# Leading groups side by side, gate products in another PSUM tile, gla levels in one call, values two pairs at a time

## The chip, the cores and the metric

The kernel runs on one core of a Trainium2 chip. The time is the device time of one execution in microseconds; a run's number is the median of its rounds. The chip's engines appear under these names: TensorE (PE, its weight loads PEld), VectorE (DVE), ScalarE (ACT), GpSimd (POOL) and SyncE (SP, which here only issues transfers).

## What is computed

Two transformer blocks in fp32 over 256 tokens of width 2048. In short form:

```python
# block 1
q_a, k_a, v_a, q_b, k_b, v_b, f_b = split(rmsnorm(x) @ w_in)
o_a = sliding window attention with sinks (16 heads of 64, 2 kv heads, window 128)
c   = cumsum(log_sigmoid(f_b + b_forget))               # the forget gates, 16 heads
o_b = softmax(q_b k_b^T / 8 + c[t] - c[s], causal) v_b  # forgetting attention, 16 heads
x   = x + rmsnorm(concat(rmsnorm(o_a), rmsnorm(o_b)) @ w_out)
x   = x + rmsnorm((gelu(gate) * val) @ w_down),  gate, val = causal_dwconv(rmsnorm(x) @ w_up)
# block 2
sb_q, sb_k, sb_v, sb_g, gla_q, gla_k, gla_v, gla_r, gla_g, sgu_u, sgu_v, sgu_g = split(rmsnorm(x) @ w_in_2)
o_sb  = stick-breaking attention          # 8 heads of 128
o_gla = gated linear attention            # 4 heads, keys of 64, decay from gla_r
o_sgu = gelu(u) * (tril(w_s) @ rmsnorm(gelu(v)) + b_s)
x = x + (rmsnorm_per_head(concat(o_sb, o_gla, o_sgu)) * silu(gates)) @ w_out_2
x = x + cross_attention(rmsnorm(x), rmsnorm(mem))
return rmsnorm(x, final_norm)
```

## The kernel before

Activations are kept transposed, with channels on partitions. All weights pass through one stream, `WeightStream`: a sub is a raw tile `wr` of 128 x up to 1024, loaded by SyncE in the order of the list `units` (L559 and on), four raw tiles deep. ScalarE makes the high half `wh` (L110), VectorE the low half `wl` (L117), three subs ahead, and `release` issues the next load once the low half is done. A wide sub carries four k-tiles of a group of 256 output channels; `ws_sub` multiplies them k-tile by k-tile, for each of the two output tiles one product of the low weights (L248, 256 columns: high inputs only) and one of the high weights (L249, 512 columns: high and low inputs). A group's first k-tile uses L245 and L246. `as_chunk` does the narrow groups with L281 to L283. The low halves of the inputs are made by VectorE in L225, and PSUM tiles `P` (two) hold the groups' sums until `join` has read them.

The order is written by hand. Everything beside the stream is a generator: `Kern.step`, called after each k-tile, counts down the generators' waits, and `yield n` means n k-tiles of pause. Within an engine instructions run in the order in which they were written, so an instruction that waits holds up all behind it on its engine.

Block 1: `attn64` makes scores into PSUM tiles `S` (L475), adds the bias on VectorE (L483), takes the exponentials (L416), transposes the weights through the one tile `T` (L434) and copies them out (L437); `values` multiplies them with V for a pair of heads into the one tile `O` (L452, L453), copies that (L455) and squares it (L463) for the group norm (`group_norm_split`, whose sum over partitions is `rms`, L328). GpSimd makes the window bias (`alibi`, L715) and scales the queries and keys (`scaled`, L317). `fox_gates` computes c by a product with a triangle U (L734 to L736), transposes it (L742), sends it to DRAM as `negc` and loads it back on all partitions into B6 and B7 (L750), which `fox_bias` reads later.

Block 2: `block2_mix` begins with two groups, `gq` and `gk` (weights w_gqk, eight subs), while the norm's residual pass still makes the inputs R (L788, L789), their high (L217) and low (L225) halves. `gla` then forms the decayed products level by level (`level`, nine levels): four products (L1124) for each of two diagonal blocks into two S tiles, then a masked copy by VectorE (L1130). The cross attention ends with the output projection; `block2_tail` sums squares by columns (`by_square`, `rms_tok`, `by_row`), multiplies R in eight steps (L1372) and stores it.

Of the kernel before, what the change touches and what calls it, by code (L numbers as in the profile page):

```python
# [16 lines left out]
P = 128  # L17
# [131 lines left out]
class Kern:  # L149
# [151 lines left out]
    def join(self, ps, ntile=2):  # L301
# [3 lines left out]
        e2 = self.t((P, 2, S), "e2")  # L305
# [48 lines left out]

    def by_square(self, sqs):

        ps = self.p("T")
        for half in range(2):
            for i, sq in enumerate(sqs):
                self.nc.tensor.matmul(ps[:, half:half + 1], sq[:, half * P:(half + 1) * P], self.ones[:, 0:1],  # L360
                                      start=i == 0, stop=i == len(sqs) - 1)
        return ps[:, 0:2]
# [39 lines left out]
    def attn64(self, pairs, qf, kf, vf, bias, sink, oraw, acc, pts, n_pts, ready, vready=None):  # L402
# [38 lines left out]
        def values():  # L441

            n = len(pairs)
            order = [2 * (h // 2) for p in pairs for h in p]
            order = sorted(set(order), key=lambda h: max(i for i, p in enumerate(pairs) if h in p or h + 1 in p))
            for i, h0 in enumerate(order):
                while not (h0 in weighted and h0 + 1 in weighted and (vready is None or self.ready[vready])):
                    yield 1
                o = self.p("O")
                for h in (h0, h0 + 1):  # L450
                    r, pt = (h % 2) * 64, weighted.pop(h)
                    nc.tensor.matmul(o[r:r + 64, 0:S], vf(h, 0), pt[:, 0:S], start=True, stop=False)  # L452
                    nc.tensor.matmul(o[r:r + 64, P:S], vf(h, 1), pt[:, S:S + P], start=False, stop=True)  # L453
                n_done[0] += 2
                nc.scalar.activation(oraw()[:, h0 // 2, :], o[:, 0:S], AF.Copy)  # L455
                if i < 2:
                    sq = acc[i]
                elif i < n - 1:
                    sq = self.t((P, S), "tc")
                else:  # L460
                    nc.vector.tensor_tensor(out=acc[0], in0=acc[0], in1=acc[1], op=ALU.add)
                    sq = acc[1]
                nc.scalar.activation(sq, o[:, 0:S], AF.Square)  # L463
                if 2 <= i < n - 1:
                    nc.gpsimd.tensor_tensor(out=acc[i % 2], in0=acc[i % 2], in1=sq, op=ALU.add)
                yield 1
# [32 lines left out]
    def group_norm_split(self, oraw, acc, gi, dst):  # L499
# [3 lines left out]
        rb = self.rms(acc, 1024, "rb")  # L503
# [20 lines left out]
    def setup(self):  # L524
# [37 lines left out]
        wide("w_gqk")  # L562
# [9 lines left out]
        nc.gpsimd.dma_start(self.gain0, a["gain0"])  # L572
        self.exp_tables()

    def block1_mix(self):
# [9 lines left out]
        for kt in range(2):  # L585
            nc.sync.dma_start(R[:, kt, :], a["xT"][:, kt, :])
            self.ws.dma()
# [11 lines left out]
        acca = [V[0][:, o + i * S:o + (i + 1) * S] for i in (1, 2)]  # L599
        accb = [V[1][:, o + P + i * S:o + P + (i + 1) * S] for i in (0, 1)]  # L600
# [72 lines left out]
        def fox():  # L673
# [12 lines left out]
            yield from self.group_norm_split(ob[0], accb, 8, dst)  # L686

        for g in range(4):
            ps = self.ws_group(x) if g else psq
            self.push(self.scaled(ps, qa[:, 2 * g:2 * g + 2, :], rq, "swa", 4))  # L690
            if g == 0:
# [3 lines left out]
                    self.group_norm_split(oa, acca, 0, dst), fox()), 8)  # L695
# [23 lines left out]
    def fox_gates(self, V):  # L719
# [13 lines left out]
        ps = self.p("T")  # L733
# [5 lines left out]
        yield 4  # L739
        ps = self.p("T")  # L740
# [5 lines left out]
        nc.gpsimd.dma_start(dr, ct)  # L746
        self.N = [self.t((P, 8, S), "B6"), self.t((P, 8, S), "B7")]
        for i in range(2):
            src = dr[8 * i:8 * i + 8, :].rearrange("a b -> (a b)").partition_broadcast(P)
            nc.gpsimd.dma_start(self.N[i].rearrange("p a b -> p (a b)"), src)  # L750
# [201 lines left out]
    def scaled_late(self, ps, dst, which):  # L952
        e = self.join(ps)
# [5 lines left out]
    def block2_mix(self):  # L959
# [6 lines left out]
        for dst, w in ((gq, "rq"), (gk, "rb")):  # L966
            ps = self.ws_group(x)
            self.push(self.scaled_late(ps, dst, w))
# [92 lines left out]
    def gla(self, G0, G1, gr, V, tg):  # L1061
# [41 lines left out]
        def level(l):  # L1103
# [17 lines left out]
            for s_, t_, slot in ((0, 0, 0), (1, 1, 2)) if l < 8 else ((0, 1, 1),):  # L1121
# [385 lines left out]
```

## Time and profile before

| | us |
|---|---|
| median of 3 runs (lowest to highest) | 1664.18 (1663.37 to 1664.45) |
| the profiled execution | 1668.66 |
| its span | 1667.0 |
| PE busy | 1638.9 (98%) |
| PEld busy | 1434.2 (86%) |
| DVE busy | 1084.0 (65%) |
| ACT busy | 934.8 (56%) |
| POOL busy | 329.5 (20%) |

The profile is one execution, and its span is what lies between its first and last instruction. A busy share is an average over the span; idle places and the granted clock are read from windows and timelines of their stretch. In a timeline row the bracket tells how long the engine was idle before the instruction and what released it.

### The profile page before, as it was taken

The page shows a single profiled execution, that of the slowest core. Times are in us where ns is not written, and L with a number is a line of the kernel's source. Part 1 is how long each engine was busy: PE and PEld are TensorE (multiplying, and loading weights), DVE is VectorE, ACT ScalarE, POOL GpSimd, SP SyncE. Part 2 cuts the span into 40 slices and gives each one's busy share as a digit, 9 for nine tenths or more (in the row PEclk, how much of TensorE's full clock was granted, in tenths as well). Part 3 has the DMA queues.
Part 4 walks back from the last instruction along what each step waited for, and adds up shares of the span by engine and source line. Part 5 has one row for each costly group of instructions (what it writes and reads, how often), then busy time and mean ns, then how long its engine had stood idle before and what let it go on. Part 6 is the DMA issues. An engine that isn't in the chain of part 4 may idle for free. (4 is left out here: it accounts for less than half of the span.)

```text
span 1667.0 us, 25018 instructions
## 1 busy us (share of the span) xinstructions
PE 1638.9 (98%) x9458; PEld 1434.2 (86%) x9458; DVE 1084.0 (65%) x1578; ACT 934.8 (56%) x1470; POOL 329.5 (20%) x270
## 2 busy tenths in 40 slices
PE   9899999999999999999999999998999999999997
PEld 8688887888888888888888888887989888888896
DVE  5677775568777777777774444448664655666766
ACT  6565565746555555555554444445545666655655
POOL 0344642211122212221220000001110322210112
PEclk9999999999999999999999999999999999999998
DMA  8545443746555555555555555654645544456652
GB/s 305 178 129 173 158 163 130 234 150 210 194 188 193 186 192 189 192 186 194 187 193 190 189 185 190 207 180 159 189 141 177 186 144 158 168 189 207 224 165 106
DMA packets 88393, 303.29 MB, mean 182 GB/s; under 512 B 9888, under 2 KB 10320, under 8 KB 87760
## 3 DMA queue, kind: packets, MB, share of 16 engines
q1 hardware_dynamic: 86976, 296.53, 52.2%
q0 software_dynamic: 1152, 4.76, 0.9%
q8 instruction: 74, 1.21, 0.3%
q14 instruction: 47, 0.39, 0.1%
q10 hardware_dynamic: 144, 0.40, 0.1%
HBM read 298.75 MB, written 2.90 MB: 181 GB/s over the span
## 5 line engine op out<-in xcount | busy, mean ns | idle before, releaser
L117 DVE TENSOR_TENSOR wl<-wr,wh 128x1024 fp32r<-128x1024 f32 (+4 forms) x546 | 687.9, 1262 | 337.3 <-ACT wh L110 336.5
L110 ACT ACTIVATE wh<-wr 128x1024 fp32r<-128x1024 f32 (+4 forms) x546 | 562.0, 1030 | 533.1 <-PE P L249 366.5
L249 PE MATMUL P<-X,wh 128*128 128x512 f32 x1852 | 649.3, 392 | 0.0
L249 PE MATMUL P<-B,wh 128*128 128x512 f32 x1668 | 590.2, 395 | 2.6 <-ACT B L217 1.4
L248 PE MATMUL P<-X,wl 128*128 128x256 f32 x1852 | 522.9, 282 | 1.4 <-ACT wh L110 1.3
L248 PE MATMUL P<-B,wl 128*128 128x256 f32 x1668 | 473.3, 284 | 1.9 <-DVE wl L117 1.9
L249 PEld LDWEIGHTS P<-X,wh 128*128 128x128 f32 x1852 | 348.5, 188 | 73.6
L249 PEld LDWEIGHTS P<-B,wh 128*128 128x128 f32 x1668 | 314.3, 188 | 74.3 <-DVE B L225 1.9
L248 PEld LDWEIGHTS P<-X,wl 128*128 128x128 f32 x1852 | 348.7, 188 | 7.0 <-issue 2.2
L248 PEld LDWEIGHTS P<-B,wl 128*128 128x128 f32 x1668 | 314.7, 189 | 5.8 <-DVE wl L117 1.7
L900 POOL TENSOR_TENSOR e<-e,rb 128x512 f32<-128x512 f32 x44 | 94.6, 2151 | 397.2 <-DVE e L309 382.3
L309 DVE TENSOR_TENSOR e<-P,e 128x512 f32<-128x512 f32 x93 | 64.2, 691 | 154.1 <-ACT e L308 150.0
L399 POOL TENSOR_TENSOR acc<-acc,tc 128x512 f32<-128x512 f32 x18 | 26.7, 1482 | 275.3 <-ACT tc L398 275.3
L281 PE MATMUL P<-wh,B 128*128 128x412 f32 (+2 forms) x192 | 68.7, 358 | 0.0
L905 ACT ACTIVATE tc<-e,cols 128x256 f32<-128x256 f32 x88 | 48.3, 597 | 34.1 <-POOL e L900 34.1
L282 PE MATMUL P<-wl,B 128*128 128x412 f32 (+2 forms) x192 | 65.0, 339 | 0.0
L283 PE MATMUL P<-wh,B 128*128 128x412 f32 (+2 forms) x192 | 65.0, 338 | 0.0
L308 ACT ACTIVATE e<-P 128x512 f32<-128x512 f32 x93 | 54.1, 582 | 9.0 <-PE P L249 6.9
L910 DVE SCALAR_TENSOR_TENSOR tc<-e,cols,tc 128x254 f32<-128x254 f32 x88 | 42.6, 484 | 3.1
L245 PE MATMUL P<-X,wh 128*128 128x512 f32 x116 | 43.5, 398 | 0.0
L908 DVE SCALAR_TENSOR_TENSOR tc<-e,cols,tc 128x255 f32<-128x255 f32 x88 | 41.8, 475 | 1.8 <-ACT tc L905 1.8
L281 PEld LDWEIGHTS P<-wh,B 128*128 128x128 f32 x192 | 36.1, 188 | 2.7 <-issue 0.3
(310 smaller groups left out, 1609.7 us busy)
## 6 DMA issues: line engine op xcount, KB each, us to landing
wr<-w_up SPq DMA_DIRECT2D x176, 512.0 KB, 4.4
wr<-w_down SPq DMA_DIRECT2D x88, 512.0 KB, 4.5
wr<-w_out SPq DMA_DIRECT2D x64, 512.0 KB, 4.5
wr<-w_qkb SPq DMA_DIRECT2D x32, 512.0 KB, 3.7
wr<-w_sb SPq DMA_DIRECT2D x32, 512.0 KB, 3.6
wr<-w_gate SPq DMA_DIRECT2D x32, 512.0 KB, 3.7
wr<-w_v SPq DMA_DIRECT2D x24, 412.0 KB, 3.2
wr<-w_v SPq DMA_DIRECT2D x16, 414.0 KB, 3.6
```

The source lines that it names most:

```text
L110: k.nc.scalar.activation(h[:, :n], src, AF.Copy)
L117: self.k.nc.vector.tensor_tensor(out=l[:, :n], in0=src, in1=h[:, :n].bitcast(F32), op=ALU.subtract)
L245: mm(o, wh, xf, start=True, stop=False)
L248: mm(o[:, 0:S], wl, xk[:, 0, :], start=False, stop=False)
L249: mm(o, wh, xf, start=False, stop=last)
L281: mm(o, xh, hh, start=kt == 0, stop=False)
L282: mm(o, xh, ll, start=False, stop=False)
L283: mm(o, xl, hh, start=False, stop=kt == KT - 1)
L308: nc.scalar.activation(e1[:, t0:t1, :], p[:, 0:t1 - t0, S:2 * S], AF.Copy)
L309: nc.vector.tensor_tensor(out=e2[:, t0:t1, :], in0=p[:, 0:t1 - t0, 0:S], in1=e1[:, t0:t1, :], op=ALU.add)
L900: nc.gpsimd.tensor_tensor(out=e, in0=e, in1=self.rb2(self.r2), op=ALU.mult)
L905: nc.scalar.activation(y[:, t, :], e[:, t, :], AF.Identity, scale=w(t, 2), bias=w(t, 3))
```

## The change

- *Gates.* `fox_gates` uses tile O for both products; the pauses are 12, 8, 4 and 6 k-tiles; its three transfers are issued by SyncE.
- *Values.* `values` takes two pairs of heads at a time in one O tile of 2 x 256, with one copy and one square of 512 columns; the norm then sums three tiles of squares (`sq_att`).
- *Head of block 2.* The eight subs of gq and gk alternate by four k-tiles, both P tiles are held, and the joins write into the destination.
- *Levels.* Both diagonal blocks of a level go into the same two S tiles in one run of eight products, with one masked copy of 512 columns per tile.
- *Tail and start.* The final norm uses `rms` with six tiles of squares instead of column sums; the scaling of the last four tiles of R moves behind it. The first gain is loaded by SyncE after the first input.

```diff
@@ join
-        e2 = self.t((P, 2, S), "e2")
+        e2 = self.t((P, 2, S), "e2") if e2 is None else e2
@@ values
-            for i, h0 in enumerate(order):
...
-                o = self.p("O")
-                for h in (h0, h0 + 1):
...
-                nc.scalar.activation(oraw()[:, h0 // 2, :], o[:, 0:S], AF.Copy)
...
-                nc.scalar.activation(sq, o[:, 0:S], AF.Square)
-                if 2 <= i < n - 1:
-                    nc.gpsimd.tensor_tensor(out=acc[i % 2], in0=acc[i % 2], in1=sq, op=ALU.add)
+            for i in range(0, n, 2):
+                hs = order[i:i + 2]
...
+                o = self.p("O").rearrange("p (a b) -> p a b", a=2)
+                for j, h0 in enumerate(hs):
+                    for h in (h0, h0 + 1):
+                        r, pt = (h % 2) * 64, weighted.pop(h)
+                        nc.tensor.matmul(o[r:r + 64, j, 0:S], vf(h, 0), pt[:, 0:S], start=True, stop=False)
+                        nc.tensor.matmul(o[r:r + 64, j, P:S], vf(h, 1), pt[:, S:S + P], start=False, stop=True)
...
+                nc.scalar.activation(oraw()[:, hs[0] // 2:hs[1] // 2 + 1:d, :], o, AF.Copy)
+                sq = acc if i == 0 else self.t((P, 2, S), "tc")
+                nc.scalar.activation(sq, o, AF.Square)
+                if i == n - 2:
+                    self.fold(acc, nc.vector)
+                    self.sq_att = [acc[:, 0, :], sq[:, 0, :], sq[:, 1, :]]
+                elif i:
+                    nc.gpsimd.tensor_tensor(out=acc, in0=acc, in1=sq, op=ALU.add)
@@ group_norm_split
-        rb = self.rms(acc, 1024, "rb")
+        rb = self.rms(self.sq_att, 1024, "rb")
@@ units
-        wide("w_gqk")
+        for i in range(2):
+            for half in range(2):
+                for g in range(2):
+                    units.append((a["w_gqk"][2 * g + i][:, 1024 * half:1024 * half + 1024], [1024], False))
...
-        nc.gpsimd.dma_start(self.gain0, a["gain0"])
@@ block1_mix
+            if kt == 0:
+                nc.sync.dma_start(self.gain0, a["gain0"])
@@ fox_gates
-        ps = self.p("T")
+        ps = self.p("O")
...
-        yield 4
-        ps = self.p("T")
+        yield 8
+        ps = self.p("O")
...
-        nc.gpsimd.dma_start(dr, ct)
+        yield 4
+        nc.sync.dma_start(dr, ct)
+        yield 6
...
-            nc.gpsimd.dma_start(self.N[i].rearrange("p a b -> p (a b)"), src)
+            nc.sync.dma_start(self.N[i].rearrange("p a b -> p (a b)"), src)
@@ block2_mix
-        for dst, w in ((gq, "rq"), (gk, "rb")):
-            ps = self.ws_group(x)
-            self.push(self.scaled_late(ps, dst, w))
+        pss = [self.big(), self.big()]
+        for i in range(0, KT, 4):
+            for ps, dst, w in ((pss[0], gq, "rq"), (pss[1], gk, "rb")):
+                self.ws_sub(ps, x, list(range(i, i + 4)), (0, KT - 1))
+                if i == KT - 4:
+                    self.push(self.scaled_late(ps, dst, w, dst))
@@ level
-            for s_, t_, slot in ((0, 0, 0), (1, 1, 2)) if l < 8 else ((0, 1, 1),):
...
-                    nc.tensor.matmul(pss[h % 2][:, h // 2 * P:(h // 2 + 1) * P], rows(k_, h)[:, s_ * P:(s_ + 1) * P],
...
-                        nc.vector.copy_predicated(a2, gm[:, l, :].unsqueeze(1).broadcast_to([P, 2, P]), ps3)
+            blocks = ((0, 0), (1, 1)) if l < 8 else ((0, 1),)
...
+                    c = (h // 2 * n + i) * P
+                    nc.tensor.matmul(pss[h % 2][:, c:c + P], rows(k_, h)[:, s_ * P:(s_ + 1) * P],
...
+                    nc.vector.copy_predicated(a2[:, :, 0:3:2, :],
+                                              gm[:, l, :].unsqueeze(1).unsqueeze(1).broadcast_to([P, 2, 2, P]), ps4)
@@ resid_evac
+            if g < 6:
+                self.sq_acc(acc, Rg, g == 0)
+            else:
+                self.sq_last = self.t((P, 2, S), "tc")
+                nc.scalar.activation(self.sq_last, Rg, AF.Square)
+                return
@@ block2_tail
-        rc, dg = self.rms_tok(self.by_square(sqs), D, "rb1c")
-        nc.scalar.activation(Rt, Rt, AF.Copy, scale=self.col("final", 15))
-        rb = self.t((P, S), "rb")
-        nc.vector.tensor_copy(rb, self.by_row(dg))
+        sqs[2:2] = [self.sq_last[:, 0, :], self.sq_last[:, 1, :]]
+        rb = self.rms(sqs, D, "rb")
+        for t in range(12, KT):
+            nc.scalar.activation(self.R[:, t, :], self.R[:, t, :], AF.Copy, scale=self.col("final", t))
```

Three places in the order of the instructions. A row is a line of the kernel, the operation, the tile written and the tiles read, with the number that tells one tile of a name from the next. First GpSimd at the gates; `td` is the window bias, `B_33` the buffer of a group of queries. Before:

```order
L715 TENSOR_SCALAR td_663<-cp_70 128x384
L715 TENSOR_SCALAR td_665<-cp_70 128x384
L746 DMA negc<-acc_691 16x256
L750 DMA B_71_697<-negc 128x2048
L750 DMA B_72_698<-negc 128x2048
L317 TENSOR_TENSOR B_33_490<-e_67_673,rq_479 128x512
L715 TENSOR_SCALAR td_770<-cp_70 128x384
```

After (the bias is L711 now):

```order
L711 TENSOR_SCALAR td_663<-cp_70 128x384
L711 TENSOR_SCALAR td_665<-cp_70 128x384
L317 TENSOR_TENSOR B_33_490<-e_67_673,rq_479 128x512
L711 TENSOR_SCALAR td_765<-cp_70 128x384
L711 TENSOR_SCALAR td_767<-cp_70 128x384
```

The queries' product now stands directly behind the two biases. The three transfers stand on SyncE, among the loads of weights; SyncE after:

```order
L89 DMA wr_716<-w_qa 128x1024
L89 DMA wr_779<-w_v 128x780
L743 DMA negc<-acc_733 16x256
L89 DMA wr_813<-w_v 128x780
L748 DMA B_83_849<-negc 128x2048
L748 DMA B_84_850<-negc 128x2048
L89 DMA wr_888<-w_v 128x780
```

Between the small transfer and the broadcasts stands one load of w_v, and behind the broadcasts the next. On TensorE at the gates, without the weight products and the repeats between; `fz` are the gates, `sm` the softmax weights. Before:

```order
L736 MATMUL T_630<-fz_516,cp_70 128x16
L475 MATMUL S_647<-B_17_95,B_33_490 128x128
L475 MATMUL S_648<-B_17_95,B_33_490 128x256
L434 MATMUL T_667<-ident_65,sm_569 128x128 x3
L742 MATMUL T_688<-ident_65,fc_634 16x128 x2
L434 MATMUL T_701<-ident_65,sm_574 128x128 x3
```

After:

```order
L732 MATMUL O_630<-fz_516,cp_70 128x16
L467 MATMUL S_647<-B_17_95,B_33_490 128x128
L467 MATMUL S_648<-B_17_95,B_33_490 128x256
L425 MATMUL T_667<-ident_65,sm_569 128x128 x3
L425 MATMUL T_688<-ident_65,sm_574 128x128 x3
L738 MATMUL O_730<-ident_65,fc_634 16x128 x2
```

The gates' products write O, and no transpose of `sm` stands behind them on the same tile. Last, TensorE at the head of block 2, the first product of each of the eight subs; the tiles B read are the inputs, four k-tiles in each, and P the sums. Before:

```order
L245 MATMUL P_10677<-B_588_10565,wh_10613 128x512
L248 MATMUL P_10677<-B_589_10566,wl_10638 128x256
L248 MATMUL P_10677<-B_590_10567,wl_10668 128x256
L248 MATMUL P_10677<-B_591_10568,wl_10704 128x256
L245 MATMUL P_10792<-B_588_10565,wh_10731 128x512
L248 MATMUL P_10792<-B_589_10566,wl_10760 128x256
L248 MATMUL P_10792<-B_590_10567,wl_10785 128x256
L248 MATMUL P_10792<-B_591_10568,wl_10819 128x256
```

After:

```order
L245 MATMUL P_10645<-B_576_10533,wh_10581 128x512
L245 MATMUL P_10646<-B_576_10533,wh_10605 128x512
L248 MATMUL P_10645<-B_577_10534,wl_10636 128x256
L248 MATMUL P_10646<-B_577_10534,wl_10673 128x256
L248 MATMUL P_10645<-B_578_10535,wl_10701 128x256
L248 MATMUL P_10646<-B_578_10535,wl_10729 128x256
L248 MATMUL P_10645<-B_579_10536,wl_10754 128x256
L248 MATMUL P_10646<-B_579_10536,wl_10783 128x256
```

Each tile of inputs is now used for both sums before the next one is read.

## Rows read from the trace of the kernel before

**Rows 1.** Windows: stretch, length, then busy PE, PEld, DVE, ACT, POOL, clock, DMA.

```profile
60.00:80.00 20.00, 15.13 (x80) 11.87 (x78) 8.91 (x29) 7.57 (x20) 8.32 (x8) 0.83 0.52 189
...
1140.00:1160.00 20.00, 18.96 (x95) 16.58 (x96) 15.46 (x24) 11.84 (x19) 0.00 (x0) 0.86 0.37 115
```

**Rows 2.** Timeline of POOL, 57 to 72 us: start, duration, instruction, idle before, releaser.

```profile
60.12 2.42 POOL L715 TENSOR_SCALAR td<-cp 128x384 f32<-128x384 f32 x2 [2.92 <-DVE mx L483]
63.59 0.59 POOL L746 DMA_DIRECT2D negc<-acc  x1 [1.04 <-DVE acc L744]
68.73 1.14 POOL L750 DMA_DIRECT2D B<-negc  x2 [4.56 <-ACT mx L419]
69.89 1.27 POOL L317 TENSOR_TENSOR B<-e,rq 128x512 f32<-128x512 f32 x1
```

**Rows 3.** Timeline of PE, 55 to 80 us, the waits and the work behind.

```profile
59.47 0.55 PE L434 MATMUL T<-ident,sm 128*128 128x128 f32 x3 [1.41 <-DVE fc L738]
...
63.34 0.55 PE L434 MATMUL T<-ident,sm 128*128 128x128 f32 x3 [1.71 <-DVE acc L744]
...
71.21 1.65 PE L475 MATMUL S<-B,B 64*128 64x128 f32 x8 [3.16 <-POOL B L317]
```

**Rows 4.** DMA issues: queue, count, KB each, median us to landing.

```profile
B<-negc POOLq DMA_DIRECT2D x2, 1024.0 KB, 8.2
```

**Rows 5.** Timeline of SP, then ACT, 68 to 92 us.

```profile
75.88 14.66 SPq L89 DMA_DIRECT2D wr<-w_v  x4
...
90.95 0.84 ACT L110 ACTIVATE wh<-wr 128x780 fp32r<-128x780 f32 x1
```

**Rows 6.** Timeline of PE: value blocks, norm, end of the group norm, gla block.

```profile
247.26 0.66 PE L452 MATMUL O<-B,B 128*64 128x256 f32 x4
...
248.06 0.39 PE L248 MATMUL P<-B,wl 128*128 128x256 f32 x1
...
249.82 0.66 PE L452 MATMUL O<-B,B 128*64 128x256 f32 x4 [0.80 <-ACT B L463]
...
265.05 1.02 PE L328 MATMUL O<-B,ones 128*128 128x256 f32 x4
...
278.00 0.36 PE L248 MATMUL P<-X,wl 128*128 128x256 f32 x1 [1.26 <-ACT wh L110]
...
1198.27 0.72 PE L1124 MATMUL S<-B 64*128 64x128 f32 x8
...
1198.92 0.45 PE L281 MATMUL P<-wh,B 128*128 128x414 f32 x1
```

**Rows 7.** Groups by shape, 1180 to 1262 us: busy, mean ns.

```profile
L1130 DVE COPY_PREDICATED B<-B,S 128x256 f32<-128x256 uint32 x32 | 12.4, 443 | 0.0
```

**Rows 8.** Timeline of DVE at the head of block 2: low weights.

```profile
1131.14 1.22 DVE L117 TENSOR_TENSOR wl<-wr,wh 128x1024 fp32r<-128x1024 f32 x1
...
1142.09 1.21 DVE L117 TENSOR_TENSOR wl<-wr,wh 128x1024 fp32r<-128x1024 f32 x1
```

**Rows 9.** Timeline of PE at the head of block 2.

```profile
1132.41 0.39 PE L248 MATMUL P<-B,wl 128*128 128x256 f32 x1 [1.40 <-DVE wl L117]
...
1158.41 0.39 PE L249 MATMUL P<-B,wh 128*128 128x512 f32 x1
...
1158.76 0.40 PE L249 MATMUL P<-B,wh 128*128 128x512 f32 x1
...
1158.99 0.35 PE L281 MATMUL P<-wh,B 128*128 128x414 f32 x1
```

**Rows 10.** Timeline: the norm of rms (DVE), then the tail (PE, DVE).

```profile
1119.86 0.42 DVE L337 SCALAR_TENSOR_TENSOR rb<-rb,rb 128x256 f32<-128x256 f32 x1
...
1653.37 0.61 PE L360 MATMUL T<-ones,acc 128*128 128x1 f32 x4 [0.80 <-POOL acc L399]
...
1658.25 4.90 DVE L1372 TENSOR_TENSOR R<-R,rb 128x512 f32<-128x512 f32 x8
```

**Rows 11.** Timeline of ACT at the start.

```profile
6.04 0.51 ACT L217 ACTIVATE X<-R,gain 128x256 fp32r<-128x256 f32 x1 [3.53 <-DMA gain<-gain]
```

## What I predicted

> **What bounds the kernel now.** I read the busy shares first: TensorE is at work in 98% of the span, and no other engine passes 65%. So a change pays only where it shortens an idle place of TensorE, a stretch at half clock, TensorE's own work, or the two ends. The windows come next: the clock falls in two inner places, around 70 us and 1140 us [rows 1]. The reader is to see that both follow idle places of TensorE, and to look in the timeline for who ended each. In the first block the gates' PSUM tile T and then GpSimd hold TensorE up [rows 2, 3]; at the head of block 2 it is VectorE, which makes the low parts of the weights [rows 8, 9].
>
> The sum is made against the profiled execution, 1668.66 us. The median of the three runs, 1664.18, is 4.5 lower; the result is moved by that.
>
> **Gates of the forgetting attention.** Before, TensorE waits 1.41 us at 59.47 and 1.71 us at 63.34, both times because tile T, which the attention's transposes want, still holds the gates' products until VectorE has read them, and 3.16 us at 71.21 for the queries that GpSimd scales in L317 [rows 3]. GpSimd issues the small transfer at 63.59, then stands in its queue until that lands, issues the two broadcasts at 68.73 and comes to L317 only at 69.89 [rows 2]. After these waits the clock is at half: a mean of 0.83 over 20 us is 6.8 us at 1.2 GHz [rows 1], and all but its first half microsecond, 6.3 us, is work of TensorE from 71.21 on [rows 3]: at full speed 3.15.
> After: the gates use O, and the transposes wait only for their own weights. I leave 0.4 us at each of the first two places for those (an estimate: VectorE's scaling of them follows TensorE's arrival closely, and T no longer delays it). On GpSimd L317 stands right behind the products that end at 62.54 [rows 2], so with its 1.27 us the queries are there at 63.8, before TensorE reaches them (about 65). So 1.41 + 1.71 + 3.16 − 0.8 = 5.5 us of waits, and 3.15 of clock: −8.65. The end that costs less is the waits alone, −5; the other is all of it, −9.5.
>
> The three transfers now stand in SyncE's queue among the weight loads. Who waits behind them: the small one waits for nothing new, but the broadcasts wait for its landing, and behind them stands the third load of w_v. SyncE's loads of w_v are issued from 75.88 on, and the first of them is converted by ScalarE at 90.95 [rows 5]; a load lands in 3 to 4 us, so some 12 us are free. The broadcasts take 8.2 us to land [rows 4]. Cover holds: cost 0; if the cover were gone it would be up to 8.2. Their readers come at about 140 us.
> The Trainium skill (DMA: Bandwidth & Descriptors, "Queues, rings and completion order") says that the DMA engines take turns between the rows of different issuers but take one issuer's descriptors in ring order. By it, the 2 MB that used to share the engines with the weights now go ahead of a load: a delay of up to the whole landing, not half of it. By either the sum stays, as the slack is longer; no row here has a transfer of that size ahead of the weights. What it would do if the slack is shorter is rival 5.
>
> **Values two pairs at a time.** A block of four value products takes from 247.26 to 248.06, 0.81 us, and the products on either side stand 0.1 us further apart than usual; the eight records by themselves would need 0.65 [rows 6]. So about 0.25 to 0.35 per block is the switch between kinds of products. Sixteen blocks become eight: −2.0. The three squares that now enter each of the two norms are one matmul more each, 0.43 from the row at 265.05 (four records and the switch, 1.02) : +0.86. In the second attention two waits shrink: 0.80 at 249.82, for the read of O [rows 6], becomes one longer read of 512 columns (ScalarE goes from 0.39 to an estimated 0.6) met half as often, and the 1.26 at 278.00 [rows 6], at the end of the group norm's chain, becomes about 0.7, as the norm starts 2 us earlier. Together −1.2. Sum −2.4; bounds: +0.5 if the longer reads stall TensorE at each of the eight blocks by 0.4, −3.5 if switching is worth 0.35.
>
> **Leading groups of block 2.** A sub (four k-tiles of a group) is eight pairs of products at 0.35 (1158.41 to 1158.76), 2.79 us [rows 9]. VectorE is busy without a break there: it makes the inputs and the low weights of the subs, whose ends are 1132.36, 1136.00, 1139.26 and 1143.30 (first and last of four in rows 8: start plus duration). Before, the q group wants all sixteen k-tiles in 11 us and waits four times, for low weights and for inputs, 4.4 us; and the clock is at half from 1138.9 to 1145.8 [rows 1, 9]. After, q and k use the same four k-tiles in turn, so the next four inputs are wanted every 5.6 us instead of 2.8, and only the low weights are waited for: the second sub starts at 1132.41 as now, the third at 1136.05 (wait 0.85), the fourth at 1139.3 (0.5), the fifth at 1143.35 (1.25), then 4 × 2.79: end 1154.5, and with the norm's matmuls that stand between 1154.9, against 1158.99 [rows 9]: −4.1. Bounds: −5 if VectorE gets ahead, −1.5 if inputs are late after all.
>
> **Levels of the gla in one call.** A block of four products takes 0.65 us from 1198.27 to 1198.92, plus 0.1 on either side; its eight records alone 0.43 to 0.45 [rows 6]. About 0.31 is the switch, and 17 blocks become nine: −2.5 (−1.5 to −3.1). VectorE's masked copy of 256 columns takes 0.44 [rows 7]; the one of 512 isn't in the trace. Bounds 0.44 (nothing more) and 0.89 (twice); either lies beside TensorE's 5.7 us a level, of which VectorE has some 2.5 spare for the two copies. Cost 0.
>
> **Tail and start.** The last product ends at 1652.4. Then sixteen one-column products wait for GpSimd's sum (0.80 at 1653.37) and a chain by columns ends at the first final product at 1658.25 [rows 10]. After: six matmuls of 0.43 from 1652.4 to 1655.0, the last on a square that ScalarE no longer does behind two scalings, then Ln, Exp and four small VectorE steps. In the same helper these took 2.4, from the end of its matmuls at 1117.87 to 1119.86 + 0.42 [rows 10]: 1657.4 to 1657.6, −0.6 (+0.3 if the last square is late, −1.0). The four scalings of R moved behind the chain, 0.42 each, end before VectorE's seventh multiplication wants them. At the start the first gain was waited for 3.53 us until 6.04 [rows 11]; through SyncE it lands some 0.7 earlier, but the whole first stage is bound by transfers, so I take −0.2 (0 to −0.7).
>
> **Sum.** −0.2 − 8.65 − 2.4 − 4.1 − 2.5 − 0.6 = −18.45: 1650.2 as a profiled execution, 1645.7 as a median.
>
> **The rivals.**
> (1) *The clock still falls at the head of block 2.* The waits left there (1.4, 0.85, 0.5, 1.25 within 13 us) look much like those after which it fell, 1.40, 0.46 and 1.37. For it: TensorE fell to 1.2 GHz without one long wait. Against it: two waits of 1.4 and 1.7 at 59 and 63 us brought no fall [rows 3]. Then one to two subs take 5.6 instead of 2.79, part of it hidden in waits: end about 1156.3, −2.3 instead of −4.1: 1647.5. The Trainium skill (TensorE: Matmul & The Clock Gate, "A second HAM failure mode: psum-queue depth-cycling") tells of a clock lost to many small idles between groups of products; by that rule this rival would come true, by the trace it is open.
> (2) *The gates' place is only half mended.* If TensorE waits there for something else (the softmax weights, which VectorE makes behind the conversions, or a value block on O), and the clock falls again, −8.65 becomes −4: 1650.3. For it: GpSimd's products before L317 themselves wait 2.92 us for VectorE at 60.12 [rows 2], so the two engines leave little slack. Against it: each of the three rows names its holder, and all three are gone. With weaker switch terms as well (values 0, levels −1.5) 1653.5.
> (3) *The change doesn't do what it says in the blocks:* the switch isn't between kinds but within each product, so eight blocks of eight cost what sixteen of four did. Then values give −0.3 instead of −2.4 and levels 0 instead of −2.5: 1650.3. Against it: in the rows the records inside a block stand closer than those at its edges [rows 6].
> (4) *Slower: the masked copy of 512.* With two broadcast dimensions VectorE might take it piece by piece. It decides from 1.25 us a copy, where VectorE's 2 copies and 3.2 of other work fill a level's 5.7; each further 0.1 costs 8 × 0.2 = 1.6 us. All 18.45 are gone at 2.4 us a copy, over five times the row of 0.44 [rows 7]; at 3 us it is 1645.7 + 28 = 1674. Against it: it reads and writes only twice the columns.
> (5) *The broadcasts starve the weights.* If the 12 us weren't there, the third load would be late by up to 8.2 us, and TensorE with it: at most 1653.9. Against it: raw tiles are loaded three subs ahead [rows 5].
>
> **How the numbers follow.** The forecast has 0.49, rival 1 0.17, rival 2 0.16, rival 3 0.08, rival 5 0.03, rival 4 0.03; 0.04 is left for little or no gain by causes that no row shows. The forecast's own bounds, −13 to −22, give 1642 to 1651; the range takes in rivals 1 to 3: 1641 to 1653.5. A measurement of this kernel can tell about 0.2%, 3.3 us, from no change. The forecast and rivals 1, 2, 3 and 5 are all faster than that: 0.93. Of the other 0.07, rival 4 and 0.01 are slower, 0.04, and 0.03 the same.
>
> **What would show it.** In the profile after: no wait on T for VectorE's fc and acc rows and none of S for L317 near 71 us, and full clock from 60 to 80 us; POOL's two queries' products back to back with td; no wait of a weight conversion on DMA near 80 to 95 us; eight value blocks and nine level blocks, with the time between them unchanged; waits at the head of block 2 on low weights alone, and its two groups over 27 us after their first product instead of 31; copies of 512 columns under 1 us; the last chain shorter by half a microsecond. Wrong would be: a new wait of ScalarE on the weight loads, a half clock at either place, or value blocks that wait on ScalarE's longer reads.

## The result and the profile after

The changed kernel takes 1651.77 us in the median of four runs (1650.81 to 1652.7) beside 1664.03 for the kernel before: 0.9923 of its time, 95% interval 0.9908 to 0.9939, 12.3 us less. I had predicted 1645.7, 18.45 us less, with a range of 1641 to 1653.5. A second set of runs gave 1651.73 beside 1665.8, ratio 0.9911 (0.9898 to 0.9925). The profiled execution of the first set takes 1650.87, where the sum had 1650.2: between the two profiled executions the step is 17.8 us, and between the medians 12 to 14. That gap is what the experiments had to settle.

From the page of the changed kernel (busy time, share of the span of 1649.2 us, instructions):

```profile
PE 1628.1 (99%) x9454; PEld 1432.4 (87%) x9454; DVE 1088.8 (66%) x1559; ACT 933.5 (57%) x1454; POOL 323.2 (20%) x259
```

From the list of what TensorE waited for (total us, count, longest):

```profile
PE P L245 <- DVE e L888: 3.9, 1, 3.9
PE P L248 <- DVE wl L117: 2.1, 2, 1.3
...
PE O L446 <- ACT B L452: 0.5, 1, 0.5
```

The gates' two waits on T and every wait for GpSimd are gone, and the largest is one that wasn't there before: the first product of gk waits 3.92 us for VectorE's L888.

**Where the trace of after stands against before.** Both kernels issue the same number of products with weights, so the start of the k-th can be compared. The differences at some landmarks, in us; e0 is a second profiled execution of the kernel before, told of below. The predicted 2.4 for the values is divided between its two rows by the step's own terms:

| stretch | predicted | before to after | e0 to after |
|---|---|---|---|
| start, to 43 us | −0.2 | −0.65 | −0.55 |
| gates and first attention's values, to 138 us | −9.25 | −9.7 | −8.1 |
| second attention's values and norm | −1.8 | −0.1 | −0.1 |
| from there to the end of block 2's head | −4.1 | −2.7 | −1.2 |
| gla levels | −2.5 | −3.2 | −3.2 |
| 1242 to 1316 us of before | 0 | −1.0 | −1.0 |
| tail | −0.6 | −0.4 | −0.5 |
| span | −18.45 | −17.8 | −14.7 |

Of the 1.2 us in the last column, 0.5 were lost by e0 alone between 300 and 600 us; they are no part of the head.

**Gates.** The windows of after (length, busy PE, PEld, DVE, ACT, POOL, clock, DMA) that answer to [rows 1]:

```profile
60.00:80.00 20.00, 20.00 (x132) 16.33 (x131) 16.07 (x48) 14.28 (x38) 10.20 (x8) 1.00 0.59 211
1110.00:1130.00 20.00, 16.08 (x76) 13.82 (x75) 19.14 (x31) 11.43 (x20) 0.58 (x1) 0.91 0.55 188
```

60 to 80 us is now full work at full clock; the half clock is at 1124 to 1127.6 us. TensorE there, for [rows 3], and GpSimd, for [rows 2]:

```profile
57.63 0.70 PE L425 MATMUL T<-ident,sm 128*128 128x128 f32 x3 [0.20 <-DVE sm L417]
...
59.57 0.49 PE L425 MATMUL T<-ident,sm 128*128 128x128 f32 x3
...
64.38 0.93 PE L467 MATMUL S<-B,B 64*128 64x128 f32 x8
```

```profile
59.50 2.42 POOL L711 TENSOR_SCALAR td<-cp 128x384 f32<-128x384 f32 x2 [2.93 <-DVE mx L475]
62.00 1.48 POOL L317 TENSOR_TENSOR B<-e,rq 128x512 f32<-128x512 f32 x1
```

The first transposes wait 0.20 for their own weights, the second ones not at all, and the scores at 64.38 don't wait: L317 stands right behind the biases and is done at 63.5. The small transfer and the broadcasts on SyncE, the third load of w_v, and its conversion by ScalarE, for [rows 5]; then the time to landing (KB each, median us) of the broadcasts and of that load:

```profile
69.75 0.42 SPq L743 DMA_DIRECT2D negc<-acc  x1
...
72.93 0.80 SPq L748 DMA_DIRECT2D B<-negc  x2
78.12 16.35 SPq L89 DMA_DIRECT2D wr<-w_v  x5
...
89.78 0.85 ACT L110 ACTIVATE wh<-wr 128x780 fp32r<-128x780 f32 x1 [0.54 <-ACT tc L452]
...
B<-negc SPq DMA_DIRECT2D x2, 1024.0 KB, 7.6
...
wr<-w_v SPq DMA_DIRECT2D x1, 390.0 KB, 4.9
```

The third load is issued at 78.12, after the broadcasts, lands 4.9 us later (the next one takes 3.5) and is converted at 89.78 without a wait for it: 6.7 us of cover are left, where I had worked out some 12. The broadcasts land in 7.6 us, beside 8.2 from GpSimd [rows 4].

**Head of block 2.** TensorE, then VectorE (for [rows 8, 9]):

```profile
1124.58 0.79 PE L245 MATMUL P<-B,wh 128*128 128x512 f32 x1 [3.92 <-DVE e L888]
...
1123.25 0.88 DVE L225 SCALAR_TENSOR_TENSOR B<-R,cols,B 128x256 fp32r<-128x256 f32 x2
1124.05 0.48 DVE L888 TENSOR_SCALAR e<-P,rmc 128x256 f32<-128x256 f32 x1
1124.44 1.22 DVE L117 TENSOR_TENSOR wl<-wr,wh 128x1024 fp32r<-128x1024 f32 x1
```

The second sum needs the second P tile, and its last user is the memory's values, whose second half VectorE copies out in L888. That copy stands in VectorE's queue behind the residual pass and ends at 1124.5. Before, gk's sum came four subs later, and the copy was never waited for. The four waits that I had worked out for the low weights are swallowed by this one.

**Levels and tail.** A block of eight products and the product behind it; the masked copies of 512 columns (count, busy, mean ns); the last product and the end of the last chain, for [rows 6, 7, 10]:

```profile
1184.68 1.16 PE L1129 MATMUL S<-B 64*128 64x128 f32 x16
1185.77 0.45 PE L281 MATMUL P<-wh,B 128*128 128x414 f32 x1
...
L1135 DVE COPY_PREDICATED B<-B,S 128x512 f32<-128x512 uint32 x16 | 11.0, 741 | 0.0
```

```profile
1634.81 0.39 PE L249 MATMUL S<-B,wh 128*128 128x512 f32 x1
...
1639.78 0.43 DVE L337 SCALAR_TENSOR_TENSOR rb<-rb,rb 128x256 f32<-128x256 f32 x1
1640.24 4.91 DVE L1381 TENSOR_TENSOR R<-R,rb 128x512 f32<-128x512 f32 x8
```

A block of eight (the profile has 16 records for them) takes 1.09 us where two of four took 1.30, and an edge of 0.2 is gone: 0.4 for each of the eight levels that have two diagonal blocks, the table's 3.2. The copy of 512 columns takes 0.74 us, between my bounds of 0.44 and 0.89. From the start of the last product to the first final multiplication it is 5.43 us, before 6.07.

### The profile page after: what moved, and what is told of

It reads as the page before. It is cut to its first block, busy times and chain, and to the rows that moved or that the text cites. A ratio compares the mean times of both kernels' runs of the same rounds, so it can differ in the third digit from the quotient of the medians.

```text
span 1649.2 us, 24946 instructions
## 1 busy us (share of the span) xinstructions
PE 1628.1 (99%) x9454; PEld 1432.4 (87%) x9454; DVE 1088.8 (66%) x1559; ACT 933.5 (57%) x1454; POOL 323.2 (20%) x259
## 5 line engine op out<-in xcount | busy, mean ns | idle before, releaser
L249 PE MATMUL P<-B,wh 128*128 128x512 f32 x1668 | 587.9, 394 | 0.1
L245 PE MATMUL P<-B,wh 128*128 128x512 f32 x100 | 38.7, 409 | 4.2 <-DVE e L888 3.9
```

The lines of the kernel that those rows point to most:

```text
L245: mm(o, wh, xf, start=True, stop=False)
L249: mm(o, wh, xf, start=False, stop=last)
```

## The experiments

All were run beside the kernel before. Its own median moved between 1664.0 and 1667.0 from one set of runs to the next, so differences are given to the changed kernel's 1651.75 (both its sets) where they are built on it. A difference "in times" is one of medians; one "in the traces" is between single profiled executions, over the same products with weights.

**e0, the kernel before profiled again.** No edit.

> The kernel before, unchanged, profiled a second time. Open: why the profiled executions differ by 17.8 us (1668.66 to 1650.87) and the medians by only 12.3 (1664.03 to 1651.77). Theory 1 (the profiler lengthens GpSimd's transfers at the gates, so the wait for L317 and the half clock behind it are longer in a profile than in an execution without one): the wait before the scores at 71 us is again about 3.2 us, the clock is again at half from 70 to 77 us, the profiled execution takes again 1667 to 1670 us. Rival 2 (that one profiled execution was an exception): a profiled execution of 1663.5 to 1665, with a shorter wait or no half clock at 70 us.

1665.62 us, span 1663.9. Two windows, and TensorE's third wait at the gates:

```profile
60.00:80.00 20.00, 15.42 (x91) 11.89 (x90) 11.33 (x30) 9.29 (x26) 8.29 (x8) 0.91 0.55 193
...
1140.00:1160.00 20.00, 20.00 (x112) 17.74 (x113) 15.93 (x26) 12.96 (x21) 1.27 (x1) 1.00 0.45 147
```

```profile
70.86 1.66 PE L475 MATMUL S<-B,B 64*128 64x128 f32 x8 [2.87 <-POOL B L317]
```

The wait is the same within 0.3 us (the other two are the same to 0.01), but the clock is at half for 3.4 us behind them instead of 6.8, and at the head of block 2 not at all (1.00 where [rows 1] has 0.86). Neither theory held as I had put it: the waits are nearly the same in both executions, the half clock behind them isn't. Every run gives its mean granted clock, and over 47 runs of the kernel before it goes with the time:

```
mean clock   0.992   0.993   0.994   0.995   0.996   0.997
runs             7       7       5      17      10       1
mean us     1668.7  1668.7  1667.5  1665.7  1664.9  1663.5
```

The first profiled execution had 0.993, so it belongs to the long end, with 14 of the 47 runs, and the three runs shown with it lay at the short one by their times. The mean is a coarse measure: in every profile kept here the clock is also at half in the last 6 to 13 us.

**e1, gates alone.**

```diff
-        ps = self.p("T")        (twice, fox_gates)
+        ps = self.p("O")
-        yield 4
+        yield 8
-        nc.gpsimd.dma_start(dr, ct)
+        yield 4
+        nc.sync.dma_start(dr, ct)
+        yield 6
-            nc.gpsimd.dma_start(self.N[i]...)
+            nc.sync.dma_start(self.N[i]...)
```

> The kernel before with the gates' part alone (tile O, SyncE, the pauses). In the profile both theories expect the same: the three waits at 59, 63 and 71 us and the half clock gone, 9.3 us less, an execution of about 1659.3. Theory 1 (the profile overstated the wait and the half clock): the timed runs gain only 4 to 5.5 us: 1658.5 to 1660. Rival 2 (the gates' gain is real without a profile too, and another part of the change loses 4 to 5 us there): the timed runs gain 9 us: 1655.

1658.75 us beside 1665.55, ratio 0.9953 (0.9939 to 0.9966): 6.8 less, between the two theories. Its window at the gates:

```profile
60.00:80.00 20.00, 20.00 (x132) 15.89 (x131) 16.59 (x56) 13.58 (x37) 9.73 (x8) 1.00 0.57 184
```

Full work at full clock. The 6.8 us are about the 5.5 us of waits and 3.4 us at half clock, which cost 1.7: what e0 shows, and not the 6.8 us at half of the first profile. In the traces the stretch from 43 to 138 us is 8.9 us shorter than in that profile and 7.3 shorter than in e0.

**e2, transfers on SyncE alone.**

```diff
-        nc.gpsimd.dma_start(dr, ct)
+        nc.sync.dma_start(dr, ct)
-            nc.gpsimd.dma_start(self.N[i]...)
+            nc.sync.dma_start(self.N[i]...)
```

> The kernel before with the gates' three transfers on SyncE alone, tile T and the pauses as before. Profile, both theories: the waits of 1.4 and 1.7 us on T stay, the one of 3.2 us for L317 and the half clock after it go, 6 us less: about 1662.5. Theory 1: timed, only 1 to 2.5 us less, 1661.5 to 1663, since without a profile the wait was short and the clock stayed up. Rival 2: timed 5.5 to 6.5 us less, about 1658.

1661.36 us beside 1665.55, ratio 0.9972 (0.9961 to 0.9984): 4.2 less, again between. The wait for L317 and the half clock are gone from its profile; left are

```profile
PE T L434 <- DVE acc L744: 1.7, 1, 1.7
PE T L434 <- DVE fc L738: 1.4, 1, 1.4
```

**e3, tile O alone.**

```diff
-        ps = self.p("T")        (twice, fox_gates)
+        ps = self.p("O")
```

> The kernel before with the gates' products in tile O alone; transfers on GpSimd and pauses as before. Theory (tile and queue are two costs that add up, and the half clock is drawn by the sum of the waits in a row): the waits of 1.4 and 1.7 us on T shrink to a few tenths, GpSimd's small transfer is issued about 1.5 us earlier and the wait for L317 stays, 2.5 to 3.5 us; 1.5 to 2.5 us less than before in the timed runs, so that tile and queue together make up the 6.8 us of both (queue alone 4.2). Rival (the wait for L317 just grows by what the tile gives): within 0.5 us of before.

1667.33 us beside 1666.67, ratio 1.0 (0.9992 to 1.0009): nothing, the rival. TensorE and GpSimd:

```profile
61.16 0.49 PE L434 MATMUL T<-ident,sm 128*128 128x128 f32 x3
...
70.94 1.65 PE L475 MATMUL S<-B,B 64*128 64x128 f32 x8 [5.11 <-POOL B L317]
...
60.87 2.42 POOL L715 TENSOR_SCALAR td<-cp 128x384 f32<-128x384 f32 x2 [2.93 <-DVE mx L483]
64.33 0.59 POOL L746 DMA_DIRECT2D negc<-acc  x1 [1.04 <-DVE acc L744]
68.49 1.10 POOL L750 DMA_DIRECT2D B<-negc  x2 [3.58 <-issue]
```

The transposes no longer wait for T, TensorE comes to the scores 2 us earlier than in e0, and then it waits 5.11 us for L317 where e0 waits 2.87. GpSimd comes to L317 at the same time (69.6 us in both), because its own chain doesn't go through T: the biases, the small transfer one microsecond behind them, the landing. So the waits on T cost nothing while the queue is there, and about 2.6 us (e1 to e2) once it isn't; the longer pauses, in which e1 and e2 also differ, weren't run by themselves.

**e4, gk's sums in the S tiles** (on the changed kernel).

```diff
-        pss = [self.big(), self.big()]
+        pss = [self.big(), self.spare()]
```

> The changed kernel with gk's sums in the two S tiles instead of the second P tile; the q group keeps P. The changed kernel's profile shows one wait of 3.92 us at the head of block 2 for VectorE's L888, which reads the previous user of that P tile (the values of the memory), and half clock from 1124 to 1127.6. Theory (the second P tile is the cause, and only the low weights are left behind it): the wait goes, waits on low weights of 1.4, 0.85, 0.5 and 1.25 us take its place as I had worked out, the two groups take 27 us instead of 28.6, 1.6 us less in the profile, and 1 to 2 us less than the changed kernel's 1651.8 in the timed runs, all at one level. Rival (VectorE's queue is the bound whatever tile is used): the same 28.6 us, with the wait put down to low weights, within 0.5 us of 1651.8.

1649.08 us (1648.81 to 1649.7), ratio to before 0.9896 (0.9881 to 0.9910), 2.7 less than the changed kernel and faster than both. TensorE's waits at the head:

```profile
1121.34 0.38 PE L246 MATMUL S<-B,wl 128*128 128x256 f32 x1 [1.18 <-DVE wl L117]
...
1124.99 0.39 PE L248 MATMUL P<-B,wl 128*128 128x256 f32 x1 [0.81 <-DVE wl L117]
...
1128.25 0.39 PE L248 MATMUL S<-B,wl 128*128 128x256 f32 x1 [0.19 <-DVE wl L117]
...
1132.30 0.39 PE L248 MATMUL P<-B,wl 128*128 128x256 f32 x1 [0.97 <-DVE wl L117]
```

1.18, 0.81, 0.19 and 0.97 us on low weights stand where I had worked out 1.4, 0.85, 0.5 and 1.25. The clock stays at full, and the four runs lie within 0.9 us of each other. The second P tile was the cause of the wait. From their first product the two groups take 27.2 us, as the prediction had it, beside 28.6 in the changed kernel and 31.1 in the kernel before. That is 1.4 of the 2.7 us; the rest no trace places.

**e5, the head as before** (on the changed kernel: the order of the subs, `block2_mix`, `scaled_late` and `join` put back).

```diff
-        pss = [self.big(), self.big()]
-        for i in range(0, KT, 4):
...
+        for dst, w in ((gq, "rq"), (gk, "rb")):
+            ps = self.ws_group(x)
+            self.push(self.scaled_late(ps, dst, w))
```

> The changed kernel with the head of block 2 as before (q group, then k group). Theory from the traces: the old head waits 4.8 us in four pieces and loses the clock in some executions only (the kernel before ran 1663.5 to 1669.2 at clocks from 0.997 down to 0.992), the new one waits 3.9 us in one piece and loses 1.7 to 3.4 us of clock in nearly all; so side by side is worth only 0 to 1.5 us as it was built: 1651.8 to 1653.3 here. By my prediction's step (4.1 us): 1655.9.

1652.42 us (1651.99 to 1653.96), 0.7 more than the changed kernel. The old head waits

```profile
1121.82 0.39 PE L248 MATMUL P<-B,wl 128*128 128x256 f32 x1 [1.40 <-DVE wl L117]
...
1125.56 0.36 PE L248 MATMUL P<-B,wl 128*128 128x256 f32 x1 [0.46 <-DVE wl L117]
1127.29 0.48 PE L249 MATMUL P<-B,wh 128*128 128x512 f32 x1 [1.37 <-ACT B L217]
...
1130.45 0.51 PE L249 MATMUL P<-B,wh 128*128 128x512 f32 x1 [1.49 <-DVE B L225]
```

That is 4.7 us in four pieces. In this profile the clock stays up behind them; three of the five runs took 1652.0 to 1652.4 us at mean clocks of 0.997 and 0.998, the others 1653.9 at 0.996. Side by side was worth 0.7 us as built, in times and in the traces; as in e4 it is worth 3.3 in times and 2.1 in the traces.

**e6, values one pair at a time** (on the changed kernel: `values`, the sums of squares and the calls of the group norm put back).

```diff
-            for i in range(0, n, 2):
+            for i, h0 in enumerate(order):
...
-        rb = self.rms(self.sq_att, 1024, "rb")
+        rb = self.rms(acc, 1024, "rb")
```

> The changed kernel with values one pair at a time (and the norms on two tiles of squares). By my prediction's step, 2.4 us more: 1654.2. By the changed kernel's trace, 0.5 us in the first attention and nothing in the second, where the group norm's chain ended no earlier on the weights' clock although it began 2 us sooner: 0.3 to 0.9 us more, 1652.1 to 1652.7.

1652.17 us (1651.89 to 1655.47), 0.4 more: less than measurement tells apart, and not the 2.4 of my step. In the traces the first attention loses 0.8 with the old values and the second 0.1. Why the second gains nothing: TensorE, VectorE and GpSimd of the changed kernel at the group norm,

```profile
252.61 0.59 PE L328 MATMUL O<-B,ones 128*128 128x256 f32 x2
...
263.28 0.35 PE L248 MATMUL P<-X,wl 128*128 128x256 f32 x1 [0.80 <-DVE wl L117]
...
267.57 0.36 PE L248 MATMUL P<-X,wl 128*128 128x256 f32 x1 [1.26 <-DVE wl L117]
...
257.53 0.96 DVE L500 TENSOR_TENSOR X<-X,rb 128x256 f32<-128x256 f32 x1
...
256.62 4.03 POOL L500 TENSOR_TENSOR X<-X,rb 128x256 f32<-128x256 f32 x4 [9.91 <-DVE rb L337]
```

the norm starts at 252.61, 2 us sooner than before on the weights' clock, but the two waits behind it come to 2.06 us. VectorE's first two multiplications overlap GpSimd's four and take 0.96 and 0.95 us; its last two, which don't, take 0.42. That this overlap is the reason is only argued here; e9 tests it.

**e7, the levels in two calls** (on the changed kernel).

```diff
-            blocks = ((0, 0), (1, 1)) if l < 8 else ((0, 1),)
...
+            for s_, t_, slot in ((0, 0, 0), (1, 1, 2)) if l < 8 else ((0, 1, 1),):
```

> The changed kernel with the gla's levels in two calls each. By my step and by the changed trace, where the levels gained 0.85 us a pair of blocks and gave back 0.45: 2.5 to 3 us more, 1654.3 to 1654.8. By rival 3 (no switch between kinds): within 0.5 us of 1651.8.

1655.1 us (1653.6 to 1656.6), 3.3 more, and 3.2 in the traces. The levels are worth somewhat more than the step's 2.5, and rival 3 falls.

**e8, the final norm by column sums** (on the changed kernel; the squares before it and the scalings of R are put back as well).

```diff
-        rb = self.rms(sqs, D, "rb")
+        rc, dg = self.rms_tok(self.by_square(sqs), D, "rb1c")
...
+        nc.vector.tensor_copy(rb, self.by_row(dg))
```

> The changed kernel with the final norm by column sums as before. By my step 0.6 us more than the changed kernel, by its trace (17.38 us gained at the last product, 17.8 at the end) 0.4 us: 1652.2. Rival (the sums of six tiles cost as much as they save): within 0.2 us; a difference this small can only be read from the profiles, from the last product to the first final multiplication: 5.8 us before, 5.4 in the changed kernel.

1653.25 us (1652.78 to 1653.77), 1.5 more. Of that the tail itself shows 0.85: the final multiplications start

```profile
1642.62 4.91 DVE L1387 TENSOR_TENSOR R<-R,rb 128x512 f32<-128x512 f32 x8
```

6.28 us after the start of the last product (1636.34), 5.43 in the changed kernel. The other 0.65 us of the medians no trace places. The two profiled executions also differ by 1.0 us near 1300 us, which has nothing to do with the edit (below).

**e9, the second group norm on VectorE alone** (on e4).

```diff
-                eng = nc.gpsimd if i % 2 else nc.vector
+                eng = nc.gpsimd if i % 2 and not gi else nc.vector
```

> The changed kernel with gk's sums in the S tiles (1649.1 us in its run), and the second group norm's eight multiplications all on VectorE instead of every other one on GpSimd. Theory (VectorE's rows of 0.96 us for a product that takes 0.42 alone show that both engines slow each other, and that this is why the chain gains nothing from its earlier start): VectorE's rows fall to 0.42, the two waits on low weights near 263 and 267 us (0.8 and 1.26) shrink by half a microsecond or more in sum: 0.5 to 1.2 us less, 1647.9 to 1648.6. Rival (VectorE has too much to do there): the same or up to 0.8 us more.

1649.2 us (1648.18 to 1650.81), as e4. In the trace the theory holds: two multiplications together take 0.75,

```profile
258.74 0.75 DVE L500 TENSOR_TENSOR X<-X,rb 128x256 f32<-128x256 f32 x2
```

and the stretch up to the weights behind the norm, counted from 42 us, is 0.9 us shorter than e4's. The next kernel, e10, has this edit too and shows the same 0.9. The median doesn't show it. Between the two profiled executions the first 42 us, before the edit has any part, differed by 1.9 us, so the effect is seen in the traces and remains unproven as a gain in time.

**e10, the memory's values copied out by ScalarE** (on e9).

```diff
-        self.nc.vector.tensor_scalar(out=out[:, 1, :], in0=ps[:, 1, 0:S], scalar1=self.rmc[:, 1:2], scalar2=None,
-                                     op0=ALU.mult)
+        self.nc.scalar.activation(out[:, 1, :], ps[:, 1, 0:S], AF.Copy, scale=self.rmc[:, 1:2])
```

> The kernel with S tiles and the norm on VectorE, and the second half of the memory's values copied out by ScalarE instead of VectorE, which frees 0.48 us of VectorE at the head of block 2 before the third sub's low weights. Theory (VectorE's queue is what the head waits for): the sum of waits there, 3.2 us with the S tiles, falls by 0.4 to 0.5, as does the time. Rival (ScalarE, which makes the high parts first, is as late): no change.

1649.24 us (1648.65 to 1650.28): no change in time. The second wait at the head is 0.43 instead of e4's 0.81; the other three are the same within 0.03:

```profile
1125.10 0.38 PE L248 MATMUL P<-B,wl 128*128 128x256 f32 x1 [0.43 <-DVE wl L117]
```

0.4 us of the head, as expected, under what the runs can tell apart.

**e11, the changed kernel again.** No edit.

> The changed kernel itself once more, as the base for the kernels that undo one part of it. Theory (the spread between executions is half clock, and the changed kernel has one place left for it, the wait of 3.92 us at the head of block 2): times between 1650.5 and 1653.5, the clock at half for 3.4 us or more behind that wait in the profile, mean clocks of 0.995 to 0.997, and a spread well under that of the kernel before (1663.5 to 1670.1 at 0.992 to 0.997). Rival (the first session's 1651.8 was low by chance, as the kernel before reads 1664.0 in one session and 1667.0 in another): 1653 to 1655.

1651.73 us (1651.22 to 1652.13), clocks 0.996 and 0.997, half clock again from 1124.7 to 1128.1. The changed kernel spreads over 2 us in nine runs, the kernel before over nearly 7.

## Why the prediction came out as it did

- **From the profiled execution to the median: this step failed.** I wrote that the median is 4.5 lower and moved the result by that. But those 4.5 us were, by e0 and the table of mean clocks, half clock for the most part, and I had also counted that half clock as saved: 3.15 at the gates, and the stretch at 1139 within the head's 4.1. Part of it was subtracted twice. Against e0, an ordinary execution, the same change is worth 14.7. That the two falls come in some executions only stood in no row that I had; the three runs, 4 to 5 us below the profiled one, were the hint.
- **The sum against the profiled execution: right to a microsecond, in part by luck** (17.8 measured, 18.45 predicted). Values, head and tail came out 3.3 us short of their terms. Start, gates and levels gave 1.6 more than theirs, and the 1.0 us between 1242 and 1316 us, which is no part of the change, made up most of the rest.
- **Gates: right in mechanism, and the clock's term held for one execution.** −8.65 predicted; 8.9 against the first profile and 7.3 against e0 in the traces (e1, and e6 the same within 0.1), 6.8 in times (e1). Rival 2, "−8.65 becomes −4", falls: nothing else is waited for and the clock stays up. Adding up 1.41, 1.71 and 3.16 was right only because all three causes went at once; e3 shows that the first two alone are worth nothing.
- **SyncE's queue: right, with less to spare.** There is no wait, and rival 5 falls, but 6.7 us of cover were left and not 12: I had taken the cover from the first load of w_v, and it is the third that stands behind the broadcasts. By the Trainium skill (DMA: Bandwidth & Descriptors, "Queues, rings and completion order") each DMA engine takes the descriptors of one ring in order. The trace doesn't decide it: the load behind the broadcasts took 4.9 us and the next 3.5, and no run here has a slack so short that the order would cost time.
- **Values: mis-sized.** −2.4 predicted, 0.4 in times and 0.9 in the traces. The switches saved are there: 0.8 us in the first attention, its norm's extra matmul paid, where the terms had 0.6. The second attention, where they had 1.8, gained 0.1: it ends in a chain that VectorE and GpSimd set, and I had priced its waits as if it began earlier and kept its length.
- **Head of block 2: the reason was right, a resource was missed.** I listed low weights and inputs as what is waited for, not who holds the PSUM tile that the second sum needs. The text says that both P tiles are held and doesn't ask who had the second. The step's 4.1 came to 2.7 against a head that had lost its clock, and to 0.7 against one that had not (e5); the missed tile cost 2.7 us in times (e4), waits and clock, of which the head's traces show 1.4. Rival 1 came true in its outcome, the clock still falls, but for one wait of 3.92 us and not for many small ones. The Trainium skill (TensorE: Matmul & The Clock Gate, "A second HAM failure mode: psum-queue depth-cycling") tells of a clock lost to small, frequent idles. The traces here go both ways: e4, with four small waits of 3.2 us together, kept the clock, and the first profile, after 1.40, 0.46 and 1.37, lost it.
- **Levels: right in mechanism, a little more than their term.** −2.5 predicted, with −3.1 as the far bound; 3.2 in the traces, 3.3 in times (e7). Rival 4 falls: 0.74 us a copy.
- **Tail: right.** −0.6 predicted, 0.4 to 0.85 in the traces.
- **The range** held the time by luck. The forecast's own bounds, 1642 to 1651, miss it by 0.8 us; the range reached further for rivals that cost as much as the error, and its reasons were others.

The parts, 6.8 for the gates put in and 0.7, 0.4, 3.3 and 0.85 (the tail, from its trace) for the others undone, come to 12.1 us, beside a difference of the medians of 12.3 to 14.1. The rest isn't settled: the start's 0.6 was not run by itself.

## What to carry to other kernels

Before a profiled execution is used as a base, compare its granted clock with that of the runs, and take the half clock out of either the base or the saving, never out of both. When sums are to be held side by side, ask of every PSUM tile who reads its last user out, and where that read stands in its engine's queue. Waits in a row on one engine add up only if they lie on one chain: take the last cause away first.

## What the runs showed of the hardware that I had not expected

- The same program falls to 1.2 GHz at one place in some executions and not in others, after nearly the same waits. In the two profiles of the kernel before the gates had 6.8 and 3.4 us at half clock, the head of block 2 had 6.8 and none. Over the 47 runs the time goes with the mean clock, by some 1.1 us for each 0.001.
- GpSimd and VectorE slow each other, and which of them gains is not the same in each execution. GpSimd's rows near 1295 us, and two conversions of weights by VectorE beside them, in the changed kernel's first profile and in its second:

```profile
1291.58 2.35 DVE L117 TENSOR_TENSOR wl<-wr,wh 128x1024 fp32r<-128x1024 f32 x2
...
1291.74 3.35 POOL L317 TENSOR_TENSOR X<-e,rq 128x512 f32<-128x512 f32 x1 [2.59 <-DVE e L309]
1295.04 0.74 POOL L1243 TENSOR_TENSOR sm<-sm,B 128x256 f32<-128x256 f32 x1
```

```profile
1291.76 3.44 DVE L117 TENSOR_TENSOR wl<-wr,wh 128x1024 fp32r<-128x1024 f32 x2
...
1291.92 2.19 POOL L317 TENSOR_TENSOR X<-e,rq 128x512 f32<-128x512 f32 x1 [2.59 <-DVE e L309]
1295.79 1.65 POOL L1243 TENSOR_TENSOR sm<-sm,B 128x256 f32<-128x256 f32 x1 [1.68 <-DVE sm L1241]
```

  GpSimd's first multiplication takes 3.35 us in the first and 2.19 in the second, VectorE's two conversions 2.35 and 3.44. Behind VectorE, GpSimd's second multiplication comes a microsecond later in the second, and TensorE then waits 0.72 us at L1056 there only. That is the 1.0 us between 1242 and 1316 us in the table. It was gained in 6 of the 14 profiled executions, of kernels with and without the change, came and went between executions of one program, and is no part of the change.
